# A ReLU row sum on one core: row blocks of 1, 97 and 30 per partition instead of 1, 111 and 16

## The chip, the core and the metric

The kernel runs on one core of a Trainium2 chip. The metric is the device time of one execution in microseconds (us). The kernel before takes 160.79 us, the median of three runs (160.78, 160.79, 161.0).

In the profile DVE is VectorE, ACT is ScalarE, and SP is SyncE, which in this kernel only issues transfers; SPq is its queue of issues. A "row" is one row of x, 1024 numbers of four bytes, 4 KB. A "partition" is one of the 128 lanes of the on-chip memory.

## The reference

The input x is 32 x 512 rows of 1024 float32, 67.1 MB. For each of the 16384 rows the kernel computes the sum of the positive entries:

```python
def reference(x: np.ndarray) -> np.ndarray:
    relu_x = np.maximum(x, 0)
    return np.sum(relu_x, axis=-1).astype(np.float32)
```

The output is 16384 numbers, 65.5 KB.

## The kernel before, in words

**Regions.** The rows are taken as one list of 16384 and given to 128 partitions, 128 rows to each. They are split into three regions (REGIONS, line 8): the first has 1 row a partition, the second 111, the third 16. Within a region a partition has consecutive rows, so the start addresses of neighbouring partitions lie 111 rows (444 KB) apart in the second region and 16 rows (64 KB) apart in the third; this distance is called the pitch below. `start` (line 44) is the first of each region's columns in `res`, the on-chip tile that holds the 128 sums of each partition; `xv` and `ov` are the regions of input and output.

**Chunks.** The input buffer `buf` has three slots of 16 rows a partition (8.39 MB each). There are seven full chunks (CHUNKS, line 9): the first is one row of region 0 and 15 rows of region 1, in two transfers, and the other six are 16 rows of region 1 each, in one transfer. Region 1's 111 rows are used up by them. The tail is region 2: transfers of 8, 4 and 2 rows (TAIL, line 12), and the last two rows of a partition, read as one run of 2048 numbers and cut into three pieces and a seam (lines 108 to 115), so that both engines can sum parts of them as they land.

**Order of the transfers.** All transfers are issued by SP in the order of lines 85 to 123 and line 207, on one queue. From the fourth chunk on each is issued when DVE has finished with the slot that it fills (s_dve, line 87); the tail is issued when the slot of the fifth chunk is free. Behind the inputs SP has three stores: the first 128 outputs (region 0, turned by DVE into rows of 32, line 117), the middle store of region 1's 111 sums a partition (line 123), and the final store of region 2's 16 sums a partition (line 207). The middle store waits for three things: `s_fact` and `s_fdve`, each raised by the last sum that ACT or DVE makes for region 1, and the landing of the last short input piece (`s_in[-1]`). The final store waits for `s_last`, which the two last sums of all raise (lines 201 and 203). The kernel ends when both region stores and the first have landed (lines 208 and 209).

**The work on a chunk.** In the first six chunks ACT writes max(x, 0) over the slot in steps of several rows (line 145) and DVE sums each step (line 160); in the sixth, four rows are left out of this and summed two by ACT and two by DVE, one instruction a row (lines 127 and 130). In the seventh chunk and the tail every row is one instruction that does both, even rows on DVE and odd rows on ACT (lines 173 to 185). Each such instruction is followed by a short read of its accumulator, which also raises the semaphore if there is one.

**Names and lines that are touched.** `row(c, i)` (line 134) gives the buffer row and the column of `res` for row i of chunk c. The loop of line 173 raises `s_fact` and `s_fdve` at the last two rows of the seventh chunk (lines 178 and 179). `rows` (line 108) is the last two rows of each partition in region 2.

Of the kernel before, what the change touches and what calls it, by code (L numbers as in the profile page):

```python
# [4 lines left out]
D = 1024  # L5
BIG = 16
NB = 3
REGIONS = [1, 111, 16]
CHUNKS = [[(0, 0, 1), (1, 0, 15)]] + [[(1, 16 * c + 15, 16)] for c in range(6)]
ACT_STEPS = [[16], [7, 9], [7, 9], [7, 9], [4, 5, 7], [3, 4, 5]]  # L10
DVE_STEPS = [[4, 5, 7], [7, 4, 5], [7, 4, 5], [7, 4, 5], [4, 5, 7], [3, 4, 5]]
TAIL = [8, 4, 2]
CUT = 912
HEAD = 256

# [1 line left out]
def bass_relu_sum_kernel(  # L17
# [19 lines left out]
    B, S, _ = x.shape  # L37
    J = B * S // P
    NBIG = len(CHUNKS)
    assert BIG * NBIG + sum(TAIL) + 2 == J == sum(REGIONS)  # L40

    xr = x.rearrange("b s d -> (b s) d")
    of = out.rearrange("b s -> (b s)")
    start = [sum(REGIONS[:i]) for i in range(len(REGIONS))]
    xv = [
        xr[P * s : P * (s + n), :].rearrange("(p j) d -> p j d", p=P)
        for s, n in zip(start, REGIONS)
    ]
    ov = [of[P * s : P * (s + n)].rearrange("(p j) -> p j", p=P) for s, n in zip(start, REGIONS)]

    buf = nc.alloc_sbuf_tensor("buf", [P, NB, BIG, D], fp32)
    w = D - CUT
    seam = nc.alloc_sbuf_tensor("seam", [P, 2 + w + HEAD + 2], fp32)
    res = nc.alloc_sbuf_tensor("res", [P, J], fp32)
    turned = nc.alloc_sbuf_tensor("turned", [P, 32], fp32)

    n_in = NBIG + len(TAIL) + 3
    s_in = [nc.alloc_semaphore(f"s_in{i}") for i in range(n_in)]
    s_act = nc.alloc_semaphore("s_act")
    s_dve = nc.alloc_semaphore("s_dve")  # L60
    s_fact = nc.alloc_semaphore("s_fact")
    s_fdve = nc.alloc_semaphore("s_fdve")
# [7 lines left out]
    sp, act, dve = nc.sync, nc.scalar, nc.vector  # L70
# [5 lines left out]
    tb = NBIG % NB  # L76
# [8 lines left out]
    for c in range(NBIG + 1):  # L85
        if c >= NB:
            sp.wait_ge(s_dve, done[c - NB])
        if c < NBIG:
            i = 0
            for g, j, n in CHUNKS[c]:  # L90
                sp.dma_start(  # L91
                    out=buf[:, c % NB, i : i + n, :], in_=xv[g][:, j : j + n, :]
# [4 lines left out]
                    arrival += 1  # L97
    r = 0
    tail = []
    for i, n in enumerate(TAIL):  # L100
        sp.dma_start(out=buf[:, tb, r : r + n, :], in_=xv[-1][:, r : r + n, :]).then_inc(  # L101
            s_in[NBIG + i], 16
        )
        tail.append((r, n, s_in[NBIG + i]))
        r += n


    rows = xv[-1].rearrange("p j d -> p (j d)")[:, r * D : (r + 2) * D]
    flat = buf[:, tb, r : r + 2, :].rearrange("p j d -> p (j d)")
    first, second, third = [(0, CUT), (D + D // 2, 2 * D), (D + HEAD, D + D // 2)]  # L110
    for k, (lo, hi) in enumerate((first, second, third)):
        sp.dma_start(out=flat[:, lo:hi], in_=rows[:, lo:hi]).then_inc(  # L112
            s_in[NBIG + len(TAIL) + k], 16
        )
# [3 lines left out]
        out=of[0:P].rearrange("(k q) -> k q", q=32), in_=turned[0:P:32, 0:32]  # L118
# [13 lines left out]
        )  # L132

    def row(c, i):
        return buf[:, c % NB, i, :], res[:, c * BIG + i : c * BIG + i + 1]

    k = 0
    for c in range(NTWO):
        alone = BIG - sum(ACT_STEPS[c])
        act.wait_ge(s_in[c], 16 * len(CHUNKS[c]))  # L140
        r = 0
# [7 lines left out]
        for i in range(BIG - alone // 2, BIG):  # L149
            on_act(*row(c, i))  # L150
        if alone:
            dve.wait_ge(s_in[c], 16 * len(CHUNKS[c]))
            for i in range(BIG - alone, BIG - alone // 2):
                on_dve(*row(c, i))
        r = seen = 0
        for n in DVE_STEPS[c]:
            if ready[r + n - 1] > seen:
# [3 lines left out]
                out=res[:, c * BIG + r : c * BIG + r + n],  # L161
                in_=buf[:, c % NB, r : r + n, :],
# [6 lines left out]
            dve.transpose(out=turned[:, :], in_=res[:, 0:32]).then_inc(s_turn, 1)  # L169


    j0 = NBIG * BIG
    for c in range(NTWO, NBIG):
        act.wait_ge(s_in[c], 16 * len(CHUNKS[c]))
        dve.wait_ge(s_in[c], 16 * len(CHUNKS[c]))
        for i in range(BIG):
            ins = (on_act if i % 2 else on_dve)(*row(c, i))
            if i >= BIG - 2:
                ins.then_inc(s_fact if i % 2 else s_fdve, 1)
    for r, n, s in tail:  # L180
        act.wait_ge(s, 16)
        dve.wait_ge(s, 16)
        for i in range(r, r + n):
            f = on_act if (i - r) % 2 else on_dve
            f(buf[:, tb, i, :], res[:, j0 + i : j0 + i + 1])

    lo, hi = first
    act.wait_ge(s_in[-3], 16)
# [3 lines left out]
    k = 2 + w  # L192
# [14 lines left out]
    sp.dma_start(out=ov[-1][:, :], in_=res[:, start[-1] : J]).then_inc(s_out, 16)  # L207
    sp.wait_ge(s_store, 16 * (len(REGIONS) - 1))
    sp.wait_ge(s_out, 16)
# [28 lines left out]
```

## Time and profile before

| what | value |
|---|---|
| median of the runs shown | 160.79 us |
| span of the profiled execution, first to last instruction | 159.4 us (159.39 in the trace) |
| time of the profiled execution around its span | not given; the median is 1.40 us above the span |
| DVE busy | 120.6 us, 76% |
| ACT busy | 101.5 us, 64% |
| input read, mean rate over the span | 67.11 MB, 421 GB/s |
| issue of the middle store | 157.08 us, 55.5 KB |
| issue of the final store | 157.93 us, 8.0 KB, 1.4 us to landing |

The times in the views count from the span's start. The page cuts the span in 40 slices of 4 us, a digit being the tenths in which an engine (or, in the line DMA, the core's 16 DMA engines on average) was busy. A timeline line gives the start, the duration, the engine, the line of the kernel, the operation, what it writes and reads, and in brackets how long the engine sat idle before it and what ended that. A line of waits names the waiting line, what it waited for, and the total, the count and the longest wait. A chain line gives the start, the duration and what the time was spent in. Besides these views the trace has a record of every DMA packet (start, duration, bytes) and of every landing, one semaphore step from each of a transfer's 16 DMA engines.

### The profile page before, as it was taken

To read this page: it belongs to the slowest core of one execution; us is meant where nothing else is said; L and a number is where in the kernel's file an instruction comes from. 1 tells how busy PE (TensorE), PEld (TensorE's weight loads), DVE (VectorE), ACT (ScalarE), POOL (GpSimd) and SP (SyncE) were. 2 spreads that over 40 slices of the span, in tenths; PEclk is the share of its full clock that TensorE was granted. 3 is DMA by queue.
4 is the path that set the end of the run, shared out by engine and by line. 5 is a ranking of instruction groups with operands and counts; after the bars stand their busy time and mean duration, and the time that the engine had idled before them with its cause. 6 is when DMAs were issued, how large, how long until landed. Compare 5 with 4: busy or idle time off the path is not lost.

```text
span 159.4 us, 150 instructions
## 1 busy us (share of the span) xinstructions
DVE 120.6 (76%) x59; ACT 101.5 (64%) x54; POOL 0.2 (0%) x4
## 2 busy tenths in 40 slices
DVE  0000000009999999999999999999999999898995
ACT  3000059980799708996099941999329980496975
POOL 0000000000000000000000000000000000000000
DMA  9997996996996997989979969969969979798994
GB/s 378 493 401 339 493 526 263 526 526 263 526 493 296 526 444 345 526 378 411 526 312 477 526 263 526 526 263 526 526 263 526 444 345 526 321 469 374 417 400 142
DMA packets 2457, 67.18 MB, mean 421 GB/s; under 512 B 536, under 2 KB 792, under 8 KB 1176
## 3 DMA queue, kind: packets, MB, share of 16 engines
q1 hardware_dynamic: 2456, 67.18, 98.1%
q14 instruction: 1, 0.01, 0.0%
HBM read 67.11 MB, written 0.07 MB: 421 GB/s over the span
## 4 chain that ended last, share of the span: by engine, by line
DVE 55%; DMA 34%; ACT 9%; SPq 2%; issue 0%
DVE res L160 54%; DMA buf<-in_x_dram 34%; ACT buf L145 9%; SPq L101 1%; SPq L112 1%; DVE buf L130 0%; DVE seam L130 0%; SPq L91 0%; DVE turned L169 0%
## 5 line engine op out<-in xcount | busy, mean ns | idle before, releaser
L160 DVE TENSOR_REDUCE res<-buf 128x4 f32<-128x4096 f32 (+3 forms) x18 | 99.4, 5596 | 35.5 <-ACT buf L145 35.5
L145 ACT ACTIVATE buf<-buf 128x7168 f32<-128x7168 f32 (+5 forms) x13 | 80.4, 6233 | 46.1 <-DMA buf<-in_x_dram 46.1
L127 ACT ACTIVATE buf<-buf 128x1024 f32<-128x1024 f32 (+2 forms) x19 | 19.0, 999 | 8.9 <-DMA buf<-in_x_dram 8.9
L130 DVE TENSOR_SCALAR_CACHE_REDUCE buf<-buf 128x1024 f32<-128x1024 f32 (+2 forms) x19 | 20.7, 1143 | 1.7 <-DMA buf<-in_x_dram 1.6
L127 ACT ACTIVATION_READ_ACCUMULATOR buf<-buf 128x1 f32 x19 | 3.6, 188 | 0.0
L145 ACT ACT_TABLE_LOAD x1 | 1.3, 1283 | 1.3 <-PEq L223 1.3
L130 DVE DVE_READ_ACCUMULATOR buf<-buf 128x1 f32 x19 | 1.6, 84 | 0.0
L130 DVE TENSOR_SCALAR_CACHE_REDUCE seam<-seam 128x258 f32<-128x258 f32 x1 | 0.4, 421 | 0.0
L127 ACT ACTIVATE seam<-seam 128x114 f32<-128x114 f32 x1 | 0.3, 300 | 0.1
L169 DVE STREAM_TRANSPOSE turned<-res 128x32 f32<-128x32 f32 x1 | 0.2, 211 | 0.0
L127 ACT ACTIVATION_READ_ACCUMULATOR seam<-seam 128x1 f32 x1 | 0.2, 186 | 0.0
L223 POOL MEMSET const-bfloat16-1.0<- 128x1 bf16 x1 | 0.1, 101 | 0.0
L223 POOL MEMSET const-uint8-127<- 128x1 uint8 x1 | 0.1, 101 | 0.0
L223 POOL MEMSET const-float32-0.0<- 128x1 f32 x1 | 0.1, 98 | 0.2 <-issue 0.2
L223 POOL MEMSET const-float32-1.0<- 128x1 f32 x1 | 0.1, 98 | 0.0
L130 DVE DVE_READ_ACCUMULATOR seam<-seam 128x1 f32 x1 | 0.1, 82 | 0.0
## 6 DMA issues: line engine op xcount, KB each, us to landing
buf<-in_x_dram SPq DMA_DIRECT2D x1, 7680.0 KB, 21.1
buf<-in_x_dram SPq DMA_DIRECT2D x1, 4096.0 KB, 25.3
buf<-in_x_dram SPq DMA_DIRECT2D x1, 2048.0 KB, 29.9
buf<-in_x_dram SPq DMA_DIRECT2D x1, 1024.0 KB, 31.9
buf<-in_x_dram SPq DMA_DIRECT2D x1, 512.0 KB, 3.3
buf<-in_x_dram SPq DMA_DIRECT2D x1, 456.0 KB, 32.5
buf<-in_x_dram SPq DMA_DIRECT2D x1, 256.0 KB, 32.7
seam<-in_x_dram SPq DMA_DIRECT2D x1, 184.0 KB, 32.6
```

The costliest lines, as they stand in the source:

```text
L101: sp.dma_start(out=buf[:, tb, r : r + n, :], in_=xv[-1][:, r : r + n, :]).then_inc(s_in[NBIG + i], 16)
L112: sp.dma_start(out=flat[:, lo:hi], in_=rows[:, lo:hi]).then_inc(s_in[NBIG + len(TAIL) + k], 16)
L127: return act.activation(t, t, AF.Relu, accum_out=acc)
L130: return dve.tensor_scalar(out=t, in0=t, scalar1=0.0, scalar2=None, op0=ALU.max, op1=ALU.add, accum_out=acc)
L145: act.activation(t, t, AF.Relu).then_inc(s_act, 1)
L160: dve.tensor_reduce(out=res[:, c * BIG + r : c * BIG + r + n], in_=buf[:, c % NB, r : r + n, :], axis=X, op=ALU.add,).then_inc(s_dve, 1)
L169: dve.transpose(out=turned[:, :], in_=res[:, 0:32]).then_inc(s_turn, 1)
L223: nc = _bacc.Bacc("TRN2", target_bir_lowering=False, num_devices=1)
```

## The change

The regions become 1, 97 and 30 rows a partition. The first six chunks still take region 0 and then region 1, which gives them 1 + 95 rows. The seventh chunk is now the first 16 rows of region 2, the tail pieces of 8 and 4 rows are its next 12, the tail piece of 2 rows is the end of region 1 (its rows 95 and 96), and the last two rows of a partition are the end of region 2. So the pitch is 97 rows (388 KB) in region 1 and 30 rows (120 KB) in region 2. Sizes, number and order of the input transfers stay.

The middle store has 97 sums a partition (388 bytes, 49.7 KB in all), and the final store 30 (120 bytes, 15.4 KB). `s_fact` and `s_fdve` are raised by the two sums of the two-row piece and no longer by the last two rows of the seventh chunk; the three conditions of the middle store are otherwise the same. `row` and the tail loop compute the columns of `res` from the regions.

```diff
-REGIONS = [1, 111, 16]
-CHUNKS = [[(0, 0, 1), (1, 0, 15)]] + [[(1, 16 * c + 15, 16)] for c in range(6)]
+REGIONS = [1, 97, 30]
+CHUNKS = [[(0, 0, 1), (1, 0, 15)]] + [[(1, 16 * c + 15, 16)] for c in range(5)] + [[(2, 0, 16)]]
...
-TAIL = [8, 4, 2]
+TAIL = [(2, 16, 8), (2, 24, 4), (1, 95, 2)]
...
-    for i, n in enumerate(TAIL):
-        sp.dma_start(out=buf[:, tb, r : r + n, :], in_=xv[-1][:, r : r + n, :]).then_inc(
+    for i, (g, j, n) in enumerate(TAIL):
+        sp.dma_start(out=buf[:, tb, r : r + n, :], in_=xv[g][:, j : j + n, :]).then_inc(
             s_in[NBIG + i], 16
         )
-        tail.append((r, n, s_in[NBIG + i]))
+        tail.append((r, n, start[g] + j, s_in[NBIG + i]))
         r += n
...
-    rows = xv[-1].rearrange("p j d -> p (j d)")[:, r * D : (r + 2) * D]
+    rows = xv[-1].rearrange("p j d -> p (j d)")[:, -2 * D :]
...
     def row(c, i):
-        return buf[:, c % NB, i, :], res[:, c * BIG + i : c * BIG + i + 1]
+        g, j, _ = CHUNKS[c][0]
+        k = start[g] + j + i
+        return buf[:, c % NB, i, :], res[:, k : k + 1]
...
-    j0 = NBIG * BIG
     for c in range(NTWO, NBIG):
         act.wait_ge(s_in[c], 16 * len(CHUNKS[c]))
         dve.wait_ge(s_in[c], 16 * len(CHUNKS[c]))
         for i in range(BIG):
-            ins = (on_act if i % 2 else on_dve)(*row(c, i))
-            if i >= BIG - 2:
-                ins.then_inc(s_fact if i % 2 else s_fdve, 1)
-    for r, n, s in tail:
+            (on_act if i % 2 else on_dve)(*row(c, i))
+    for r, n, j, s in tail:
         act.wait_ge(s, 16)
         dve.wait_ge(s, 16)
-        for i in range(r, r + n):
-            f = on_act if (i - r) % 2 else on_dve
-            f(buf[:, tb, i, :], res[:, j0 + i : j0 + i + 1])
+        for i in range(n):
+            f = on_act if i % 2 else on_dve
+            ins = f(buf[:, tb, r + i, :], res[:, j + i : j + i + 1])
+            if start[1] <= j < start[2] and i >= n - 2:
+                ins.then_inc(s_fact if i % 2 else s_fdve, 1)
```

## The prediction on record

> **What bounds the kernel now.** I read the page's slices and queue line first, then the chain that ended last in order of time, then the timeline of the last 22 us, then SP's own waits, and last the trace's records of single DMA packets and semaphore landings.
>
> ```profile
> DMA  9997996996996997989979969969969979798994
> ...
> q1 hardware_dynamic: 2456, 67.18, 98.1%
> ...
> DVE 55%; DMA 34%; ACT 9%; SPq 2%; issue 0%
> ```
>
> The chain's summary names DVE, but that is only one of two parallel tellings: DVE runs without a gap from 35.5 us, and so does the DMA queue. What decides is the middle line: packets of the one input queue fill 98.1% of what 16 engines have in 159.4 us. The transfers of 8.39 MB land 19.35 us apart (ACT's starts behind them: 40.97, 60.31, 79.67, 99.02, 118.36), which is 433 GB/s, and stay so whichever engine is busy. So the input stream sets 157.0 us of the span; what follows it is a short tail:
>
> ```profile
> 124.39 32.60 DMA buf<-in_x_dram
> 156.99 0.02 issue
> 157.01 0.44 DVE buf L130 x2
> 157.45 0.02 issue
> 157.47 0.43 DVE seam L130 x2
> ```
>
> The last lines of the chain: the stream, one short sum at 157.01, the two sums over the seam at 157.47, which wait for the seam's own transfer (its sixteen landings end at 157.44). Behind that chain stand the two stores and the pieces that free them:
>
> ```profile
> 154.84 1.06 ACT L127 ACTIVATE buf<-buf 128x1024 f32<-128x1024 f32 x1 [0.32 <-DMA buf<-in_x_dram]
> 154.84 1.22 DVE L130 TENSOR_SCALAR_CACHE_REDUCE buf<-buf 128x1024 f32<-128x1024 f32 x1
> 155.80 0.19 ACT L127 ACTIVATION_READ_ACCUMULATOR buf<-buf 128x1 f32 x1
> ...
> 155.98 0.08 DVE L130 DVE_READ_ACCUMULATOR buf<-buf 128x1 f32 x1
> ...
> 157.08 0.34 SPq L123 DMA_DIRECT2D out_dram<-res  x1
> ...
> 157.93 0.34 SPq L207 DMA_DIRECT2D out_dram<-res  x1
> ```
>
> The first four are the two-row piece (one row on ACT, one on DVE); the fifth issues the middle store, the sixth the final one. SP's waits say which condition of each store came last:
>
> ```profile
> SPq L122 <- DMA buf<-in_x_dram: 31.0, 1, 31.0
> ...
> SPq L209 <- DMA out_dram<-res: 1.1, 1, 1.1
> ```
>
> The middle store waits for the last piece of input (s_in[-1]), not for ACT or DVE. The last 1.1 us are the landing of the final store.
>
> **The change part by part.**
>
> *Instructions and queues.* SP still issues 18 transfers in the same order behind the same waits; ACT and DVE keep the same number, shapes and order of sums. Only the addresses read, the columns of res written, the bytes of two stores, and the two instructions that raise s_fact and s_fdve differ. No engine gets or loses work: 0.
>
> *Release of the middle store, moved from the last sums of the last full chunk to those of the two-row piece.* In the trace of before the old sums raise their semaphores at 146.16 and 146.94 us; the two-row piece ends at 155.80+0.19 = 155.99 on ACT and 155.98+0.08 = 156.06 on DVE. The other condition, s_in[-1], comes at 156.99. So the new release is 156.99-156.06 = 0.93 us early and costs 0. What is queued behind this wait on SP is only the final store (L207), which itself waits until 157.93, and the issue takes 0.34: another 0.5 us could pass before that is late. If that cover were gone, each us of delay would cost one.
>
> *Middle store, 97 sums (388 B a partition) instead of 111 (444 B).* Its 128 packets of 444 B took 24 ns each, eight to an engine; they run from 157.93 to 158.25 and land by 158.69, while the final store lands from 159.17 to 159.35. Saving 8 x 3 ns (12.6% of 24) there is hidden by the 0.66 us between the two landings: 0.
>
> *Final store, 30 sums (120 B) instead of 16 (64 B).* This stands on the path. The trace has no 120 B piece on this path, so I bound it by the rows beside it. 64 B: 10.4 ns a packet, sixteen landings over 0.175 us, 0.38 us from the last data packet's end (158.97) to the last landing (159.35). 444 B: 24 ns, over 0.217 us, 0.43 us (158.25 to 158.69). Treating 120 B as 444 B would cost 8 x 13.6 ns = 0.11, plus 0.04, plus 0.05: 0.20 us. The lower end is 0, since more bytes in the same number of packets have no reason to be quicker. By bytes it lies (120-64)/(444-64) = 15% of the way, close to the 64 B row: **+0.03 us**. Its 128 pieces now begin at multiples of 120 B, not of 64 B; those of 444 B were no better aligned, so the upper end covers that.
>
> The Trainium skill (DMA: Bandwidth & Descriptors, How a descriptor splits into AXI transactions) speaks against the change here: a transaction starts at a 256 B boundary, so pieces at multiples of 64 B never cross one and pieces at multiples of 120 B often do. By that page I count 8 beats of 32 B on average for a 120 B piece against 5 for a 64 B one, at its 850 MHz an estimate of 8 x 3 x 1.18 ns = 0.03 us an engine. The sum is no different by it; no run here shows the beats.
>
> *Input addresses.* The pitch between partitions goes from 444 KB (111 rows) to 388 KB (97 rows) for the first six chunks and for the two-row piece (there from 64 KB), from 444 KB to 120 KB (30 rows) for the last full chunk, from 64 KB to 120 KB for the rest of the tail. The trace of before holds both a wide and a narrow pitch: a 64 KB packet at 444 KB pitch took 2.418 us at the least and 2.421 on average, a 32 KB packet at 64 KB pitch took 1.213 in all 128 cases, a 16 KB one 0.611, an 8 KB one 0.310. All lie on one line, 8 ns a packet plus 36.8 ns per 1000 bytes: the address shows nowhere. Value: 0. Where it could show is the start: of the 128 packets of 60 KB in the first transfer from the long region 25 took more than 2.30 us where the shortest took 2.267, 2.46 us too much in all, or 0.15 an engine; the worst took 2.547. So the ends are -0.15 (all of that goes) and +0.28 (the engine that is last meets one more such packet).
>
> The Trainium skill (same page, Latency and other measured facts, HBM row pitch at large powers of two) lists slower copies at pitches of 512 KiB and above, 207 GB/s against 214 when padded. Stretched to the 64 KB pitch of the last 16 rows a partition (8.39 MB, 19.4 us) that 3% would be a gain of 0.6 us, an estimate. By the row it is 0: 4.19 MB at that pitch took 9.71 us, half of a full chunk's 19.35 is 9.68. The row decides.
>
> *Sum.* 0 + 0 + 0 + 0.03 + 0 = +0.03 us on a span of 159.39, giving 159.42. The profile gives no separate time of its own execution; the median of the runs shown, 160.79, stands 1.40 us above the span, and nothing that the change touches lies there. 159.42 + 1.40 = **160.82**, said as 160.8.
>
> **Rivals.**
>
> *Slower by the new pitch.* The 97-row pitch lets packets queue in memory. An engine moves 8 packets of 60 KB and 40 of 64 KB from the long region; from 7 ns each (2.425 instead of 2.418) the cost passes 0.32 us. At 2.427, where the slowest tenth of before lies, it is 48 x 9 ns = 0.43: 161.2. For it: the first 10 us show that engines can hold each other up. Against: 1.213 in all cases at the narrowest pitch.
>
> *Slower by the final store.* 120 B pieces share lines of memory with their neighbours and land late. Bounded by the 444 B row it is 0.20, so 161.0, within no change; it decides only if one landing takes 0.32 us longer than now, nearly twice 0.38: 161.1 or more. The middle store, with the same sharing, speaks against it.
>
> *Slower by the release.* The two-row piece would have to end 0.93 us later, and SP's 0.5 us be used up as well. At twice that piece's 1.2 us it would end near 157.3, past s_in[-1] but inside SP's slack. Price below 0.1: 160.9.
>
> *Faster by the pitch of the tail.* Against a full chunk's rate the tail's pieces take more: 9.71 - 9.68, 4.89 - 4.84, 2.51 - 2.42, and 2.62 - 2.42 to the seam's landing at 157.44, together 0.37 us. Were all of it the 64 KB pitch: 160.4. But the packet line above gives that to the 8 ns of each packet and the spread of sixteen engines, which stay.
>
> **How the numbers follow.** A measurement of this kernel can tell about 0.2% from no change, 0.32 us: same means 160.47 to 161.11. Forecast 0.81; slower by pitch 0.07, by the final store 0.03, by the release 0.01; faster by the pitch 0.08. The release's price would stay within the bound, so same is 0.82, slower 0.10, faster 0.08. Range: the forecast with its unknowns reaches down 0.15 and up 0.20 + 0.28 if both come; the three runs themselves span 0.22 above their lowest. I take 160.5 (the fast case's near edge) to 161.15 (the two upper ends are unlikely to meet).
>
> **What would show it.** Right: landings of full chunks still 19.35 us apart; the last input at 157.0 +- 0.3; L123 still behind the input's wait, at about 157.1; final store 1.4 to 1.45 us from issue to landing. Wrong: 64 KB packets at 2.425 or more; tail pieces at 9.68, 4.84 and 2.42; a final landing 0.3 us longer; SP's L122 waiting for ACT or DVE.

## The result and the profile after

The changed kernel takes 161.05 us, the median of 20 runs (160.89 to 161.76); the kernel before, run beside it, 160.83 us (160.72 to 161.11, 20 runs). The ratio is 1.0015, with an interval from 1.0008 to 1.0022. So the change costs 0.22 us, less than the 0.2% (0.32 us) that the prediction took as the bound, but more than nothing. The forecast was 160.8, no change; the range 160.5 to 161.15 holds the time. The profile shows the cost in two places, of which the prediction had priced one at 0.03 us and the other at 0; whether the other comes in every execution is taken up at run 11.

The span grew from 159.39 to 159.64 us. The first view is the queue line of the page, then the end of the chain of waits in order of time (start, duration, what):

```profile
q1 hardware_dynamic: 2456, 67.18, 98.0%
```

```profile
124.44 32.67 DMA buf<-in_x_dram
157.10 0.02 issue
157.13 0.44 DVE buf L130 x2
157.57 0.02 issue
157.59 0.43 DVE seam L130 x2
```

The input still fills the queue, and the chain has the same links. The last short input piece now ends at 157.10 where it ended at 156.99: **0.12 us later, the first part**. From there the links are as long as before (0.44, 0.43). The timeline of the same stretch shows the two-row piece, which now frees the middle store, and both stores:

```profile
154.94 1.22 DVE L130 TENSOR_SCALAR_CACHE_REDUCE buf<-buf 128x1024 f32<-128x1024 f32 x1
154.94 1.06 ACT L127 ACTIVATE buf<-buf 128x1024 f32<-128x1024 f32 x1 [0.30 <-DMA buf<-in_x_dram]
155.90 0.18 ACT L127 ACTIVATION_READ_ACCUMULATOR buf<-buf 128x1 f32 x1
...
156.08 0.08 DVE L130 DVE_READ_ACCUMULATOR buf<-buf 128x1 f32 x1
...
157.19 0.35 SPq L123 DMA_DIRECT2D out_dram<-res  x1
...
158.05 0.34 SPq L208 DMA_DIRECT2D out_dram<-res  x1
```

The new release comes at 156.16 (156.08 + 0.08), 0.94 us before the input's end, as predicted; the middle store goes out 0.09 us after that end, as before. SP's waits agree:

```profile
SPq L122 <- DMA buf<-in_x_dram: 31.1, 1, 31.1
...
SPq L210 <- DMA out_dram<-res: 1.2, 1, 1.2
```

The middle store still waits for the input alone, and the wait for the final store's landing went from 1.1 to 1.2. In the landing records it is exact: from the issue of the final store to its last landing 1.417 us before, 1.553 after: **0.136 us, the second part**. 0.12 + 0.136 is the 0.25 us of the span.

The second part is seen in single landings. A landing is one step of the store's semaphore, one for each of 16 DMA engines. Before, the sixteen of the final store come in an even row, 11 or 12 ns apart, 1.242 to 1.417 us after the issue. After, they begin at 1.275, come 11 or 12 ns apart but for one step of 25 ns, stop at 1.382 for 101 ns, and go on from 1.483 to 1.553. The packets themselves cost what was forecast: 12.5 ns each instead of 10.4, the last data packet 1.067 us after the issue instead of 1.036. So of the 0.136 us 0.03 is packets, and the rest lies between the last packet and the last landing: 0.49 us instead of 0.38.

### The profile page after: what moved, and what is told of

Read it like the earlier page. It is cut to its first block, busy times and chain, and to the rows that moved or that the text cites. A ratio compares the mean times of both kernels' runs of the same rounds, so it can differ in the third digit from the quotient of the medians.

```text
span 159.6 us, 150 instructions
## 1 busy us (share of the span) xinstructions
DVE 120.6 (76%) x59; ACT 101.5 (64%) x54; POOL 0.2 (0%) x4
## 4 chain that ended last, share of the span: by engine, by line
DVE 55%; DMA 34%; ACT 9%; SPq 2%; issue 0%
DVE res L162 54%; DMA buf<-in_x_dram 34%; ACT buf L147 9%; SPq L101 1%; SPq L112 1%; DVE buf L130 0%; DVE seam L130 0%; SPq L91 0%; DVE turned L171 0%
```

## The experiments

The theories are: **S**, the final store lands later for the form of its pieces (length, or how they lie in memory); **P**, the new pitch between partitions makes the stream end later; **N**, both shifts are scatter of single executions. S was later split in **A**, pieces that share a short run of memory with their neighbours, and **B**, length. To part them, most of the kernels have store sizes that are free of the input regions:

```diff
+STORE = [1, 97, 30]
-    ov = [of[P * s : P * (s + n)].rearrange("(p j) -> p j", p=P) for s, n in zip(start, REGIONS)]
+    ost = [sum(STORE[:i]) for i in range(len(STORE))]
+    ov = [of[P * s : P * (s + n)].rearrange("(p j) -> p j", p=P) for s, n in zip(ost, STORE)]
...
-    sp.dma_start(out=ov[1][:, :], in_=res[:, start[1] : start[2]]).then_inc(s_store, 16)
+    sp.dma_start(out=ov[1][:, :], in_=res[:, ost[1] : ost[2]]).then_inc(s_store, 16)
...
-    sp.dma_start(out=ov[-1][:, :], in_=res[:, start[-1] : J]).then_inc(s_out, 16)
+    sp.dma_start(out=ov[-1][:, :], in_=res[:, ost[-1] : J]).then_inc(s_out, 16)
```

The results together; "final store" is the time from its issue to its last landing and "pause" the longest step in its row of landings, both from the one profiled execution of each kernel, and "last input" is the end of the last short input piece there. The ratio is to the kernel before in the same job, which had medians of 160.87, 160.92 and 160.88 us in the three jobs (runs 1 to 4, 5 to 8, 9 to 12).

| kernel | median us | ratio, interval | last input us | final store us | pause ns |
|---|---|---|---|---|---|
| before | 160.83 | | 156.99 | 1.417 | 12 |
| changed | 161.05 | 1.0015, 1.0008 to 1.0022 | 157.10 | 1.553 | 101 |
| 1 stores alone, 120 B at 120 B | 160.97 | 1.0007, 0.9998 to 1.0016 | 157.04 | 1.564 | 111 |
| 2 inputs alone, 64 B at 64 B | 160.90 | 1.0004, 0.9995 to 1.0012 | 157.15 | 1.479 | 76 |
| 3 final 128 B at 128 B | 160.87 | 0.9996, 0.9987 to 1.0005 | 157.03 | 1.425 | 14 |
| 4 final 64 B at 120 B | 160.93 | 1.0003, 0.9994 to 1.0012 | 157.04 | 1.506 | 82 |
| 5 final 448 B at 448 B | 161.03 | 1.0009, 1.0000 to 1.0018 | 157.00 | 1.559 | 13 |
| 6 final 444 B at 444 B | 161.16 | 1.0021, 1.0011 to 1.0030 | 157.09 | 1.695 | 115 |
| 7 final 8 B at 8 B | 162.65 | 1.0111, 1.0096 to 1.0126 | 157.07 | 3.326 | 299 |
| 8 final 120 B at 128 B | 160.88 | 1.0000, 0.9990 to 1.0009 | 157.18 | 1.431 | 12 |
| 9 pitch 128 rows | 161.26 | 1.0023, 1.0013 to 1.0032 | 157.58 | 1.557 | 52 |
| 10 pitch 127 rows | 161.10 | 1.0011, 1.0001 to 1.0021 | 157.18 | 1.419 | 12 |
| 11 inputs of the change, final 128 B | 160.99 | 1.0004, 0.9995 to 1.0012 | 157.16 | 1.425 | 12 |
| 12 blocks of 1, 95 and 32 | 160.97 | 1.0007, 0.9998 to 1.0015 | 157.85 | 1.431 | 12 |

**Run 1, the stores alone.** The kernel before with STORE = [1, 97, 30].

> The input addresses, the sums and the semaphores of the kernel before; only the two last stores are cut as in the change, 97 and 30 sums a partition, so that the sums land at other places of the output than the reference's. Theory S (the final store's longer pieces, which no longer begin at multiples of 64 B, make it land later): from its issue to the end of the span 1.55 us as in the profile after, against 1.43 before, a median 0.1 to 0.25 us above the kernel before. Theory P (the new pitch between partitions makes the stream end later): last input at 157.0, the median within 0.08 of the kernel before. Theory N (both shifts are scatter of single executions): no run differs by more than 0.08.

The final store takes 1.564 us, with a pause of 111 ns, as in the changed kernel, although the inputs are those of before; the last input is at 157.04. The issue lines of its trace (KB of 1024 bytes, and us from issue to landing where the trace has it) against 1.4 before:

```profile
out_dram<-res SPq DMA_DIRECT2D x1, 48.5 KB
...
out_dram<-res SPq DMA_DIRECT2D x1, 15.0 KB, 1.6
```

The second line is the final store. The median is 0.10 us above that of before; the interval just takes in 1. So the store's part goes with the stores, not with the inputs.

**Run 2, the inputs alone.** The changed kernel with STORE = [1, 111, 16].

> The changed kernel with the stores cut as before, 111 and 16 sums a partition, so that the sums land at other places of the output than the reference's. Theory S: final store 1.43 us from issue to the end, the median within 0.08 us of the kernel before. Theory P: the last input at 157.1 or later, the mean 64 KB packet at 2.423 us or more against 2.421, the median 0.1 to 0.25 above the kernel before. If S and P each hold one half: about 0.1 above here and in the run with the stores alone.

The last input is at 157.15, as theory P has it, but the mean 64 KB packet took 2.4216 us, which is that of before and not 2.423. The final store took 1.479, more than before and less than with 120 B: there is a pause of 76 ns with pieces of 64 B at 64 B too. The median is 0.03 above before, and the ratio's 1.0004 is not told from 1. Neither theory has it as it said; the inputs' part stays small and open. Runs 1 and 2 together make 0.13 us by the medians and 0.0011 by the ratios, of the change's 0.22 and 0.0015; what is missing lies within the intervals.

**Run 3, 128 B at multiples of 128 B.** STORE = [1, 95, 32], inputs of before.

> The kernel before with stores of 95 and 32 sums a partition: the final store's pieces are 128 B at multiples of 128 B (the sums land at other places of the output than the reference's). If in theory S it is the alignment of the pieces that costs: like the kernel before within 0.05 us, the final store 1.43 us from issue to the end. If it is their length: like the run with 120 B pieces or a little more, 1.55 us and 0.1 to 0.25 above. Under P and N no difference.

1.425 us and no pause, though a piece is longer than 120 B; median 160.87, equal to before. The times agree with the landings: run 3 and run 1 were timed in one job, have the same inputs and differ only in how the two stores are cut, and the eleven runs of run 3 lie at 160.77 to 160.93, those of run 1 at 160.91 to 161.15. So the 0.1 us of run 1 is the stores' layout, and a piece that is a little longer need not cost.

**Run 4, 64 B at a distance of 120 B.** STORE = [1, 97, 30], and

```diff
-    sp.dma_start(out=ov[-1][:, :], in_=res[:, ost[-1] : J]).then_inc(s_out, 16)
+    sp.dma_start(out=ov[-1][:, 0:16], in_=res[:, J - 16 : J]).then_inc(s_out, 16)
```

> The kernel before with a middle store of 97 sums, and a final store of only the last 16 sums a partition, at a distance of 120 B in the output: 64 B pieces that no longer begin at multiples of 64 B. 14 sums a partition are not stored, and the rest land at other places than the reference's. If in theory S the alignment costs: like the run with 120 B pieces, 1.5 to 1.55 us from issue to the end, 0.1 to 0.25 above the kernel before. If the length costs: like the kernel before, 1.43 us and within 0.05. Under P and N no difference.

The store took 1.506 us with a pause of 82 ns, at the edge of what alignment was to cost, with the packets as short as before. The median moved by 0.06, which the interval does not tell from none. It counts for alignment and against length, but weakly.

**Runs 5 and 6, the same length with and without sharing.** STORE = [1, 15, 112] and STORE = [1, 16, 111].

> The kernel before with stores of 15 and 112 sums a partition: final pieces of 448 B at multiples of 448 B, so each begins and ends at a multiple of 64 B (the sums land at other places than the reference's). Theory A (what costs is a piece that begins or ends inside a run of 64 B that it shares with the next partition's piece, since 128 B pieces at multiples of 128 B took 1.425 us from issue to last landing, 120 B pieces 1.553 and 1.564): the last landing follows the last data packet by 0.36 to 0.40 us with no gap over 30 ns in the row of landings, and only the packets' own time is longer, 8 x 13.6 ns: 1.52 to 1.58 us from issue. Theory B (length costs): 0.45 us or more after the last packet.

> The kernel before with stores of 16 and 111 sums a partition: final pieces of 444 B at multiples of 444 B, which share a run of 64 B with their neighbours (the sums land at other places than the reference's). Theory A: gaps of 70 ns or more in the row of landings, the last one 0.45 us or more after the last packet, 0.06 us or more later than the 448 B pieces. Theory B: as the 448 B pieces within 0.03 us.

Both moves of theory A came: 448 B landed in an even row, 0.39 us after the last packet, and 444 B paused for 115 ns, 0.53 us after the last packet. The issue lines of the final stores, of run 5 and of run 6:

```profile
out_dram<-res SPq DMA_DIRECT2D x1, 56.0 KB, 1.6
```

```profile
out_dram<-res SPq DMA_DIRECT2D x1, 55.5 KB, 1.7
```

The smaller store is the slower one, by 0.136 us in the landings and 0.13 us in the medians (161.16 against 161.03, in one job; the intervals of the two ratios overlap).

**Run 7, 8 B pieces.** STORE = [1, 97, 28, 2].

> The kernel before with a middle store of 97 sums and a final store of 2 sums a partition: 8 B pieces, eight of which share each run of 64 B. 28 sums a partition are not stored and the others land at other places than the reference's. Theory A: a gap of 70 ns or more, at least 1.5 us from issue to last landing, though the pieces are the shortest of all; if each sharing costs, more than the 120 B pieces' 1.56. Theory B: 1.40 us or less, the best of all.

This is the run that decides against length. The shortest store of all is by far the slowest: the landings come up to 299 ns apart and the last one 3.326 us after the issue. In its waits of SP and its issue line:

```profile
SPq L211 <- DMA out_dram<-res: 3.0, 1, 3.0
```

```profile
out_dram<-res SPq DMA_DIRECT2D x1, 1.0 KB, 3.3
```

1.0 KB takes longer to land than 56 KB. Its data packets took 8.6 ns each and were through 1.03 us after the issue, as in the kernel before; the other 2.3 us lie behind them. The median is 1.73 us above before, so the profile's reading is the time's too. Theory B, which had 1.40 us, falls. That sharing is the reason is less certain here than for the other runs: 8 B pieces that lie far apart were not run, so the shortness of a piece, and the one KB in which all 128 lie, remain as rivals for the size of this cost.

**Run 8, 120 B that share nothing.** STORE = [1, 95, 32], and

```diff
-    sp.dma_start(out=ov[-1][:, :], in_=res[:, ost[-1] : J]).then_inc(s_out, 16)
+    sp.dma_start(out=ov[-1][:, 0:30], in_=res[:, J - 30 : J]).then_inc(s_out, 16)
```

> The kernel before with a middle store of 95 sums and a final store of 30 sums at a distance of 128 B in the output: pieces of 120 B that begin at multiples of 128 B and share no run of 64 B with another piece, but fill their last run in part. 2 sums a partition are not stored and the others land at other places than the reference's. If in theory A the sharing costs: as the 128 B pieces, 1.43 us from issue to last landing, no gap. If a run filled in part costs: 1.5 us or more with a gap, as the 120 B pieces at 120 B. Theory B: as the 120 B pieces within 0.03.

The pieces of the change, only spread to multiples of 128 B, land 1.431 us after the issue without a pause, and the ratio is 1.0000:

```profile
out_dram<-res SPq DMA_DIRECT2D x1, 15.0 KB, 1.4
```

The same 15.0 KB took 1.6 in run 1. So, by the landings, it is neither the length nor a run that is filled in part at its end; the medians of runs 1 and 8, from two jobs with overlapping intervals, do not decide it by themselves. What is left is how the pieces lie, and theory A puts that down to sharing. One rival was not run: that a piece costs if it begins inside a run of 64 B, whoever else writes there. The stores whose pieces share such runs (the change, runs 1, 6 and 7) have pieces that begin so, and run 4 has them without sharing and paused as well; pieces that begin so and lie too far apart to share even 128 B were not run. How long the shared run is stays open: with runs of 64 B run 4 should have had no pause, since its pieces share none, and run 2 none either. Pieces that share no run of 128 B never paused (runs 3, 8, 11, 12); of those that share one of 128 B but none of 64 B some did (runs 2, 4 and 9) and some did not (before, runs 5 and 10).

**Runs 9 and 10, wider pitches.** All inputs but the first transfer from a block of PITCH rows a partition, 128 or 127, with the stores of before:

```diff
+PITCH = 128
-        xr[P * s : P * (s + n), :].rearrange("(p j) d -> p j d", p=P)
-        for s, n in zip(start, REGIONS)
+        xr[0:P, :].rearrange("(p j) d -> p j d", p=P),
+        xr[0 : P * PITCH, :].rearrange("(p j) d -> p j d", p=P),
```

> The kernel before with its stores; every input after the first transfer is read at a pitch of 128 rows, 512 KB, a power of two (a partition reads 127 rows from a block of 128, so other rows are summed than in the reference). Theory P (the pitch between partitions sets how packets hold each other up): the stream differs by much more than in the change, the 64 KB packets above 2.43 us, the last input after 157.3, the median 0.3 us or more above the kernel before. Theory N (the pitch is nothing, the 0.1 us of the changed kernel's stream was scatter of the start): last input between 156.98 and 157.10, where the kernels with the addresses of before lie, the median within 0.1.

> The same at a pitch of 127 rows, 508 KB (other rows are summed than in the reference). Theory P: between the power of two and the kernel before, at most 0.15 above the latter, as the last input at 157.10 and 157.15 is with 97 and 30 rows. Theory N: last input between 156.98 and 157.10, the median within 0.1.

At 512 KB the stream does end later, at 157.58, and the median is 0.38 us up; but the 64 KB packets are not at 2.43, they took 2.422 on average. The loss is all at the start. The timeline of run 9 (ACT's first work, behind the first chunk's landing, and its next), then that of the kernel before, from which run 9 is made, then that of the changed kernel:

```profile
22.26 13.86 ACT L148 ACTIVATE buf<-buf 128x16384 f32<-128x16384 f32 x1 [19.71 <-DMA buf<-in_x_dram]
...
41.60 13.95 ACT L148 ACTIVATE buf<-buf 128x7168 f32<-128x7168 f32 x2 [5.49 <-DMA buf<-in_x_dram]
...
60.96 6.18 ACT L148 ACTIVATE buf<-buf 128x7168 f32<-128x7168 f32 x1 [5.40 <-DMA buf<-in_x_dram]
```

```profile
21.61 13.86 ACT L145 ACTIVATE buf<-buf 128x16384 f32<-128x16384 f32 x1 [19.06 <-DMA buf<-in_x_dram]
...
40.97 13.95 ACT L145 ACTIVATE buf<-buf 128x7168 f32<-128x7168 f32 x2 [5.50 <-DMA buf<-in_x_dram]
...
60.31 13.95 ACT L145 ACTIVATE buf<-buf 128x7168 f32<-128x7168 f32 x2 [5.39 <-DMA buf<-in_x_dram]
```

```profile
21.67 13.86 ACT L147 ACTIVATE buf<-buf 128x16384 f32<-128x16384 f32 x1 [19.12 <-DMA buf<-in_x_dram]
...
41.05 13.95 ACT L147 ACTIVATE buf<-buf 128x7168 f32<-128x7168 f32 x2 [5.53 <-DMA buf<-in_x_dram]
...
60.41 6.18 ACT L147 ACTIVATE buf<-buf 128x7168 f32<-128x7168 f32 x1 [5.40 <-DMA buf<-in_x_dram]
```

The first chunk lands 0.65 us later than before and 0.59 later than in the changed kernel, and from there all three run in step: 41.60 to 60.96 and 41.05 to 60.41 are 19.36 each, 40.97 to 60.31 is 19.34. At the last input 0.59 of the 0.65 us is left. This one execution took 161.50 us, 0.24 above the median of run 9, so 0.65 is more than the usual loss, and its final store took 0.14 us more than that of before, so not all of the median's 0.38 need be the start. Of the first large transfer's 60 KB packets 38 took more than 2.30 us in run 9, 10.0 us too much in all and 3.43 the worst, against 25 and 2.46 us before and 23 and 4.08 in the changed kernel. At 508 KB the median is 0.22 us up, at the lower edge of its interval 0.02; that is more than either theory had (0.15 and 0.1), and the one profile, with its last input at 157.18, does not show where the time goes. So the pitch can act, in run 9's profile at the start of the stream only; with 97 and 30 rows its size is not shown by these two.

**Run 11, the inputs of the change with a clean store.** The changed kernel with STORE = [1, 95, 32].

> The input addresses of the change with stores of 95 and 32 sums, so that the final store's pieces are 128 B at multiples of 128 B (the sums land at other places than the reference's). It takes the store's cost out of the change and leaves the inputs. Theory P: last input at 157.10 to 157.15, the final store 1.43 us from issue to last landing, the median 0.05 to 0.12 above the kernel before. Theory N: last input as with the addresses of before, median within 0.04. The whole cost of the change in the store alone would give the latter.

The last input at 157.16 and the store at 1.425 fit theory P; the median is 0.11 above before, while the paired ratio is 1.0004 and takes in 1, as in run 2. The end of its chain of waits:

```profile
157.16 0.02 issue
157.18 0.44 DVE buf L132 x2
157.62 0.02 issue
157.64 0.43 DVE seam L132 x2
```

The inputs of the change ended at 157.10, 157.15 and 157.16 in three profiles. Those of before ended between 156.99 and 157.18 in eight (six of them below 157.08). The shift of about 0.1 us is likely but not shown. Where it arises can be read from the landings: from the first chunk's last landing to the last short input piece it is 135.39 to 135.45 us in these three profiles and 135.38 to 135.45 in the eight, so nothing is lost behind the first chunk. That chunk lands at 21.65, 21.72 and 21.77 with the inputs of the change, at 21.58 to 21.79 with those of before; the two overlap.

**Run 12, blocks of 1, 95 and 32.** The changed kernel with another cut, the middle store freed by the last full chunk as before:

```diff
-REGIONS = [1, 97, 30]
+REGIONS = [1, 95, 32]
...
-TAIL = [(2, 16, 8), (2, 24, 4), (1, 95, 2)]
+TAIL = [(2, 16, 8), (2, 24, 4), (2, 28, 2)]
...
-            (on_act if i % 2 else on_dve)(*row(c, i))
+            ins = (on_act if i % 2 else on_dve)(*row(c, i))
+            if i >= BIG - 2:
+                ins.then_inc(s_fact if i % 2 else s_fdve, 1)
...
-            if start[1] <= j < start[2] and i >= n - 2:
-                ins.then_inc(s_fact if i % 2 else s_fdve, 1)
```

> Row blocks of 1, 95 and 32 a partition with all sums stored in their places: pitch 95 rows (380 KB) in the middle region and 32 rows (128 KB) in the last, final store 128 B a partition at multiples of 128 B, the middle store released by the last full chunk as before. Theory S with A (sharing of 64 B runs): 1.43 us from issue to last landing; it takes back the store's part of the change, 0.1 us, so 0.1 to 0.2 below the changed kernel. Under theory P something of the inputs' 0.1 stays; under N it equals the kernel before within 0.05. No theory makes it faster than the kernel before by more than 0.05.

The store lands 1.431 us after the issue, without a pause. The median is 160.97, 0.09 above before with a ratio that takes in 1; it lies 0.08 below the changed kernel, in another job, a little less than the 0.1 to 0.2 that was expected. Its profiled execution is its longest (161.64 us against 160.82 to 161.20 of the eleven others): its 64 KB packets took 2.430 us on average, 111 of 768 over 2.44, spread over the stream, where the other kernels have 2.421 to 2.423. What held them up the trace does not tell; such an execution is also what makes the changed kernel's few runs of 161.5 to 161.8 possible, which is not shown. No version was faster than the kernel before.

## Why the prediction was right, and which term was mis-sized

*What bounds the kernel.* Right, and the reason why so large a rearrangement costs next to nothing: the stream sets the time. The queue is filled to 98.0%, chunks land 19.36 us apart, and no engine's work moved.

*Release of the middle store: 0.* Right. The piece ends at 156.16 and the input at 157.10: 0.94 us of cover, 0.93 forecast. SP's wait at L122 names the input.

*Middle store: 0.* Right in effect, with two wrong numbers. Its packets took 23.6 ns instead of 24.0, a smaller saving than the 3 ns that the prediction took. And the prediction read only twelve of the sixteen landings of the middle store before: they end not at 158.69 but at 159.05, 1.967 us after its issue, so the cover was 0.30 us (to 159.35) and not 0.66. In the profile after they end at 159.05 as well, 1.860 us after the issue, and the final store at 159.60: still hidden, by 0.55.

*Final store: +0.03, ends 0 and 0.20.* This is the term that was mis-sized: 0.136 in the profile, 0.10 in the median of run 1. It lies inside the ends. The landing after 1.553 us also lies outside the 1.4 to 1.45 us that the prediction named as a sign of being right. The value failed because it was taken by bytes, 15% of the way from the 64 B to the 444 B row. The runs put in its place a step: what a final store of 444 B has over one of 64 B behind its last packet is not its length, since 448 B did not have it (0.39 us from last packet to last landing in run 5, 0.53 in run 6), and pieces of 120 B at multiples of 120 B have most of it (0.49 us). The prediction said that the 444 B pieces "were no better aligned, so the upper end covers that", and had a likely cause in hand; it should have picked the row by alignment and not by length. Read in full, that row gave a hint: the middle store of before landed with steps of 84 and 318 ns, and 0.79 us after its last packet (158.25 to 159.05), not 0.43. It is a hint and no more, since the same store had no step over 36 ns in runs 2 and 10. The upper end read from it would have been some 0.5 us (0.11 of packets, 0.79 - 0.38 of landing). The end of 0.20 also counts something twice: the time from the last packet to the last landing (0.05 more) already holds the longer row of landings (0.04), so that reading gives 0.16. That 0.136 stayed under the end of 0.20 is in part luck, as that end came from a row read in part.

*The Trainium skill (DMA: Bandwidth & Descriptors, How a descriptor splits into AXI transactions).* The estimate of 0.03 us an engine by its 256 B boundary is near what the packets gained (12.5 - 10.4 ns, eight times, 0.02), but not for its reason: 120 B packets took 12.5 ns at multiples of 128 B too (run 8), and 64 B packets 10.5 ns at multiples of 120 B (run 4), so where they begin did not show in their time. It has nothing of the 0.1 us behind the last packet, and 128 B pieces, two to each 256 B, did not pay that. Here the measurement decides.

*Input addresses: 0, ends -0.15 and +0.28.* Inside the ends; the profile after has +0.12, two more profiles with these inputs +0.16 and +0.17 against the same profile before, and the timed pair of runs 2 and 11 a ratio of 1.0004 each, about 0.06 us, with intervals that take in 1. Whether the value of 0 was wrong stays open. The place that the prediction named, packets of the first large transfer that are held up, is the one that run 9 shows at a larger pitch (10.0 us of excess against 2.46).

*The Trainium skill (same page, Latency and other measured facts, HBM row pitch at large powers of two).* The page has a lower rate at a per-partition pitch of 512 KiB, in copies between HBM tensors. Run 9 has that pitch for nearly all of its input: its 64 KB packets took 2.422 us against 2.421, so the rate is the same, and what its profile shows it to pay is 0.65 us once, at the start. The page's 3% would have been an estimate of 4.7 us on 157.

*Rivals.* "Slower by the final store" had the mechanism that the runs point to, pieces that share memory with their neighbours, with a chance of 0.03 for more than 0.32 us; it came with 0.136 and stayed within the bound. It was held to be unlikely since the middle store had "the same sharing", but read in full, the middle store's landings do not speak against it. "Slower by the new pitch" wanted 2.425 us a packet, and 2.423 was measured; its 7 ns count from the shortest packet, 2.418, and from the mean, 2.421, the sign should have been 2.428. "Faster by the pitch of the tail" did not come: the pieces of 8, 4 and 2 rows landed 9.74, 4.86 and 2.49 us after the one ahead, at pitches of 120, 120 and 388 KB, against 9.71, 4.89 and 2.51 at 64 KB.

## What to carry to other kernels

Look at how a final store lies in memory before its length: pieces of 128 B at multiples of 128 B, or of 120 B at such multiples, landed without a pause here, pieces of 120 B side by side paused for 0.1 us, and a store of 8 B from each of 128 partitions cost more than a large one. Price an unknown operation by the row that shares its form, not by the one that is nearest in size, and read all of that row's landings. And where a stream fills the queue, read single packets and landings: in these runs the start and the last landing are where an address showed.

## What the runs showed of the hardware that was not expected

A store of 1.0 KB in 8 B pieces took 3.33 us from issue to last landing, while 56 KB in 448 B pieces took 1.56; the packets of the first were done after 1.03 us. The sixteen landings of an undisturbed final store come 11 to 14 ns apart, 0.175 to 0.178 us from first to last. A pitch of 512 KB between partitions cost 0.65 us in the first chunk of run 9's profile and nothing in the following ones.
